# Transposes of a four-layer decoder trunk moved from TensorE to the DMA crossbar, and a second PSUM bank for gate and up

## The chip, the cores and the metric

One core of a Trainium2 chip. The time is device microseconds of one execution of the whole kernel; the figure of a kernel is the median of its runs. The profile comes from one more execution, under the hardware profiler.

## The reference

A decoder trunk of four layers on x of 256 rows and 1024 columns, all in float32. Layer i uses the mixer i mod 3, so the order is A, B, C, A:

```python
for i in range(DEPTH):                       # DEPTH 4
    hn = rms_norm(x, norm_gains[i, 0])
    m = mixer(hn)                            # A, B or C
    x = x + rms_norm(m, norm_gains[i, 1])
    f = swiglu(rms_norm(x, norm_gains[i, 2]), w_gate[i], w_up[i], w_down[i])   # hidden 2816
    x = x + rms_norm(f, norm_gains[i, 3])
# A: differential attention, 8 heads of two 64-wide maps, rotary positions, values 128 wide:
#    wts = softmax(q0 k0) - lam * softmax(q1 k1);  o = rms_norm(wts @ v, subln_g) * (1 - lam_init);  o @ w_out
# B: stick-breaking attention, 16 heads of 64, strictly causal:
#    a = exp(log_sigmoid(z) + sum over later keys of log_sigmoid(-z));  (a @ v) @ w_out
# C: sliding window of 128, 16 query heads on 2 key heads, learned sinks
```

## The kernel before

The 256 rows are two streams of 128 rows (s = 0 and 1). Both run the same program, `stream(s)`, as Python generators: a norm, the mixer, `out_proj`, a norm, `ffn`, a norm. Weights come in units of 128 x 1024 floats (512 KB), 378 in all. Each unit is loaded by SyncE's queue into one of STAGE = 4 buffers (`load_dma`, L247 and L251), split by ACT and DVE into a high and a low part (`hi`, `lo`), and held in a ring of 11; a product is three matmuls, high x high, high x low and low x high. Both streams use a unit once, so stream 0 may be at most LAG = 8 units ahead.

The class `Emitter` writes the order of the program: it keeps a clock of the matmul time emitted so far, lets the generators run in turn, and a generator says when it may go on: `("w",)` for the next weight unit, `("d", ns)` for a delay on that clock, `("e", key)` for an event that another sets. Work beside the main line (turning q, k, scores, values) is spawned as a task. After the first stretch the tile framework may still move an instruction ahead of one that waits. Nearly every instruction is recorded under one helper's line, L182, so the profile is read by tile names.

PSUM has 8 banks of 128 x 512 floats: for each stream one `tp` (transposes, values), one `mm` (projections), two `acc` (scores, output and down products, and the first chunk of a projection). Short-lived SBUF tiles share one ring of TMP = 8 buffers of 2 KB a partition (tag `t2k`).

A and B work in two groups g of four head pairs. For each group the units of q, k and v are projected in chunks of 512 columns (tiles `mm_a000q`: mixer, layer, stream, group, part). q and k are turned so that the head dimension lies on partitions: `four_transposes` makes four f32 transposes on TensorE into `tp` (tiles `tt_...`) and ACT copies them out (`qT`, `kT`). The scores (`sc_`) go through softmax or the stick-breaking scan in two steps of two; the weights of a step are turned the same way (`tw_`, `ta_`, copied to `wT`, `aT`), then the values are taken (`pv_`). A also normalises the output of each head and turns it (`on_`, `to_`). `split_rows` splits the result for `out_proj` (`acc_a`, `acc_b`), whose rows 0 to 3 come from the first group and 4 to 7 from the second.

`ffn` goes over 11 chunks of 256 hidden columns: `project` puts gate and up of a chunk side by side in one bank (`acc` for chunk 0, else `mm`; tile `mm_f`), ACT and DVE form h, h is turned, and `down` multiplies it into two `acc` banks (`acc_f`). Down of chunk c follows the projection of chunk c + 1; chunks 8, 9 and 10 come at the end. Except for the last chunk, h is turned by DMA, in `turned_by_dma` (L566): the crossbar moves two-byte elements, so GpSimd first copies the 32-bit words into planes of low and high halves (`hp`), SyncE's queue issues the transpose (`hq`), and GpSimd joins the halves (`hx`).

The gains of the two post norms of a layer are loaded for all partitions (`load_gain`, L447) into two buffers in turn, when stream 0 first needs them named.

Of the kernel before, what the change touches and what calls it, by code (L numbers as in the profile page):

```python
# [9 lines left out]
F32 = mybir.dt.float32  # L10
F32R = mybir.dt.float32r
BF16 = mybir.dt.bfloat16
I32 = mybir.dt.int32
U16 = mybir.dt.uint16
# [5 lines left out]
P = 128  # L20
D = 1024
# [13 lines left out]
TMP = 8  # L35
# [123 lines left out]
def trunk_kernel(ctx, tc, x, positions, norm_gains, a_w_in, a_w_out, a_lambda, a_subln, b_w_in, b_w_out,  # L159
# [285 lines left out]
    def load_gain(i, n):  # L445
        t = wk.tile([P, D], F32, tag="gain", name=f"gain_{i}_{n}")
        nc.sync.dma_start(t, norm_gains[i, n].partition_broadcast(P))  # L447
        return t

    gain_tiles = {}  # L450

    def gain_of(i, n):
        if (i, n) not in gain_tiles:
            gain_tiles[i, n] = load_gain(i, n)
        return gain_tiles[i, n]
# [40 lines left out]
    def project(s, xn, n, units_, name, first):  # L496

        b = bank("acc" if first else "mm", s, [P, n], f"mm_{name}")
        per = KT // units_
        for u in range(units_):  # L500
            w = yield ("w",)
            js = [(per * u + j, slice(j * n, (j + 1) * n)) for j in range(per)]
            for kt, cs in js:
                for v in range(2):
                    mm(b, xn[0][:, kt, :], w[v][:, cs], kt == 0 and v == 0, False)
            for kt, cs in js:
                mm(b, xn[1][:, kt, :], w[0][:, cs], False, kt == KT - 1)
        return b
# [52 lines left out]
    def turned_by_dma(h, name):  # L561

        planes = wk.tile([P, 2, 256], U16, tag="t2k", name=f"hp_{name}", bufs=TMP)
        pool.tensor_copy(planes, h.bitcast(U16).rearrange("p (n w) -> p w n", w=2))
        tq = wk.tile([P, 4, P], U16, tag="t2k", name=f"hq_{name}", bufs=TMP)
        nc.sync.dma_start_transpose(tq, planes.rearrange("p w n -> p (w n)"))  # L566
        t = wk.tile([P, 2, P], F32, tag="t2k", name=f"hx_{name}", bufs=TMP)
        pool.tensor_copy(t.bitcast(U16).rearrange("p b (t w) -> p w b t", w=2), tq.rearrange("p (w b) t -> p w b t", w=2))
        return t
# [14 lines left out]
    def layer_a(s, i, xn):  # L584
# [7 lines left out]
        def turned(chunk, g, which):  # L592
            t = rope(chunk, 8, *tabs[which], f"{name}{g}{which}")
            yield ("d", 2000)
            dst = None
            if which == "k":
                dst = kT[g, s] = wk.tile([P, 4, P], F32, tag=f"kT{g}{s}", name=f"kT_{name}{g}", bufs=1)
            else:
                dst = qT[g] = queries(s, 4, f"{name}{g}")
            four_transposes(s, t.rearrange("p h d -> p (h d)"), dst, f"tt_{name}{g}{which}")  # L600
            em.set((name, which, g))
            if which == "k":
                yield from scores(g)

        def scores(g):
# [8 lines left out]
            for step in range(3):  # L614
# [23 lines left out]
                if step > 0:  # L638
                    if step == 2:
                        yield ("d", 1500)  # L640
                    tp = bank("tp", s, [P, 2, nk, P], f"tw_{name}{g}{step}")
                    for h in range(2):
                        for kb in range(nk):
                            transpose(tp[:, h, kb, :], ws[step - 1][:, h, kb * P:(kb + 1) * P])
                    act.activation(wT[g][:, 2 * step - 2:2 * step], tp, AF.Copy)
                    yield ("d", 300)
# [4 lines left out]
        def values(g):  # L651
# [17 lines left out]
            tp = bank("tp", s, [P, 4, P], f"to_{name}{g}")  # L669
            for h in range(4):  # L670
                transpose(tp[:, h, :], on[:, h, :])
# [19 lines left out]
    def layer_b(s, i, xn):  # L691
# [6 lines left out]
        def turned(chunk, g, which):  # L698
# [8 lines left out]
            four_transposes(s, t, dst, f"tt_{name}{g}{which}")  # L707
# [4 lines left out]
        def scores(g):  # L712
# [6 lines left out]
            for step in range(3):  # L719
# [23 lines left out]
                if step > 0:  # L743
                    if step == 2:
                        yield ("d", 1500)
                    for p in range(2):
# [122 lines left out]
    def ffn(s, i, xn):  # L869
# [8 lines left out]
        def down(c):  # L878
            nonlocal acc
            for j in range(2):  # L880
# [6 lines left out]

        for c in range(NCH):
            chunk = yield from project(s, xn, 512, 4, f"{name}{c}", c == 0)
# [5 lines left out]
            if c == NCH - 1:  # L895
                yield from down(c - 2)
                yield from down(c - 1)
            elif c in (0, NCH - 2):
                yield ("d", 2200)
            else:  # L900
                yield from down(c - 1)
            if c == NCH - 1:
                t = bank("tp", s, [P, 2, P], f"th_{name}{c}")
                for j in range(2):
                    transpose(t[:, j, :], h[:, j * P:(j + 1) * P])
            else:
                t = turned_by_dma(h, f"{name}{c}")
            if c % 2 == 0:
                hT[c] = hT[c + 1] = [wk.tile([P, 4, P], F32R, tag=f"o{q}{s}", name=f"hT{q}_{name}{c}") for q in "hl"]
            split_rows(hT[c], slice(2 * (c % 2), 2 * (c % 2) + 2), t)  # L910
# [4 lines left out]
    def stream(s):  # L915
        if s:
            yield ("d", 1500)
        for i in range(depth):
# [6 lines left out]
            gain = gain_of(i, 1)  # L925
            oT, name = yield from (layer_a, layer_b, layer_c)[kind](s, i, xn)
            acc = yield from out_proj(s, oT, name, (1, 1, 3)[kind])
            post_norm(s, acc, gain, f"m{i}{s}")
            yield ("d", 4000)
            gain = gain_of(i, 3)  # L930
# [3 lines left out]
            post_norm(s, acc, gain, f"e{i}{s}")  # L934
            if i < depth - 1:
                yield ("d", 4000)
# [30 lines left out]
```

## Time and profile before

| | |
|---|---|
| median of 3 runs | 1188.63 us (1187.36 to 1189.47) |
| profiled execution | 1192.19 us, of which 1190.4 from first to last instruction |
| granted TensorE clock | 0.997 |
| TensorE (PE) busy | 1168.0 us (98%) |
| VectorE (DVE) busy | 779.4 us (65%) |
| ScalarE (ACT) busy | 649.0 us (55%) |
| GpSimd (POOL) busy | 175.0 us (15%) |
| moved by DMA | 216.42 MB, 182 GB/s in the mean |

PE stands for TensorE's matmuls (transposes among them), PEld for its weight loads, SP for SyncE. Matmuls are pipelined, so two of them overlap in the busy time, and what one costs the engine is read from start to start. A name in a row is that of the tile written, then, behind the arrow, those of the tiles read. The number behind x is a count. In a row of waits the numbers are total us, times, and where there is a third, the longest. In a timeline row they are start and length in us, and in brackets the engine's idle time before the instruction and what ended it.

### The profile page before, as it was taken

The page shows a single profiled execution, that of the slowest core. Times are in us where ns is not written, and L with a number is a line of the kernel's source. Part 1 is how long each engine was busy: PE and PEld are TensorE (multiplying, and loading weights), DVE is VectorE, ACT ScalarE, POOL GpSimd, SP SyncE. Part 2 cuts the span into 40 slices and gives each one's busy share as a digit, 9 for nine tenths or more (in the row PEclk, how much of TensorE's full clock was granted, in tenths as well). Part 3 has the DMA queues.
Part 4 walks back from the last instruction along what each step waited for, and adds up shares of the span by engine and source line. Part 5 has one row for each costly group of instructions (what it writes and reads, how often), then busy time and mean ns, then how long its engine had stood idle before and what let it go on. Part 6 is the DMA issues. An engine that isn't in the chain of part 4 may idle for free.

```text
span 1190.4 us, 16818 instructions
## 1 busy us (share of the span) xinstructions
PE 1168.0 (98%) x5868; PEld 958.5 (81%) x5868; DVE 779.4 (65%) x1217; ACT 649.0 (55%) x1197; POOL 175.0 (15%) x301
## 2 busy tenths in 40 slices
PE   8999999999999999999999999999999999999997
PEld 7787888888878888888888878888877888888776
DVE  7876765565847666666588676556686777655553
ACT  5665654444756665444476664444465666534542
POOL 2000122221200012111110012111110001211211
PEclk9999999999999999999999999999999999999999
DMA  8635467877743546777663256777764454677661
GB/s 278 211 124 161 147 193 195 225 211 216 233 135 125 177 145 196 213 208 226 207 203 125 90 158 201 210 209 212 217 207 144 139 162 130 193 205 215 192 194 40
DMA packets 184361, 216.42 MB, mean 182 GB/s; under 512 B 53074, under 2 KB 148436, under 8 KB 184276
## 3 DMA queue, kind: packets, MB, share of 16 engines
q1 hardware_dynamic: 183568, 215.00, 60.8%
q8 instruction: 46, 0.75, 0.3%
q10 hardware_dynamic: 708, 0.34, 0.1%
q14 instruction: 39, 0.32, 0.1%
HBM read 203.76 MB, written 1.05 MB: 172 GB/s over the span
## 4 chain that ended last, share of the span: by engine, by line
PE 68%; DMA 10%; DVE 7%; POOL 5%; ACT 5%; issue 4%; SPq 0%; POOLq 0%; ACTq 0%; DVEq 0%
PE mm_f L182 26%; PE acc_f L182 12%; DMA hq_f<-hp_f 8%; DVE lo L182 4%; PE acc_a L182 3%; POOL hp_f L182 3%; ACT hi L182 2%; PE mm_c L182 2%; PE acc_b L182 2%; PE sc_a L182 2%; POOL hx_f L182 1%; PE acc_c L182 1%; DMA stage<-in_a_w_in_dram 1%; PE sc_b L182 1%; PE pv_a L182 1%
## 5 line engine op out<-in xcount | busy, mean ns | idle before, releaser
L182 DVE TENSOR_TENSOR lo<-stage,hi 128x1024 fp32r<-128x1024 f32 x378 | 457.6, 1224 | 130.3 <-ACT hi L182 127.6
L182 ACT ACTIVATE hi<-stage 128x1024 fp32r<-128x1024 f32 x378 | 393.8, 1056 | 124.9 <-PE mm_f L182 49.9
L182 PE MATMUL mm_f<-hi,xh_q 128*128 128x512 f32 x704 | 275.8, 392 | 2.3 <-DVE h_f L182 2.3
L182 PE MATMUL mm_f<-lo,xh_q 128*128 128x512 f32 x704 | 274.8, 390 | 0.0
L182 PE MATMUL mm_f<-hi,xl_q 128*128 128x512 f32 x704 | 217.5, 390 | 1.0 <-DVE xl_q L182 1.0
L182 ACT ACTIVATE hTh_f<-hx_f 128x256 fp32r<-128x256 f32 x80 | 33.4, 418 | 229.4 <-POOL hx_f L182 229.4
L182 PEld LDWEIGHTS mm_f<-hi,xh_q 128*128 128x128 f32 x704 | 132.6, 188 | 30.9 <-ACT t_f L182 2.4
L182 PEld LDWEIGHTS mm_f<-hi,xl_q 128*128 128x128 f32 x704 | 132.4, 188 | 29.5 <-DVE xl_q L182 1.8
L182 PEld LDWEIGHTS mm_f<-lo,xh_q 128*128 128x128 f32 x704 | 132.6, 188 | 27.4 <-DVE lo L182 0.2
L182 DVE TENSOR_TENSOR hTl_f<-hx_f,hTh_f 128x256 fp32r<-128x256 f32 x80 | 34.0, 425 | 162.9 <-ACT hTh_f L182 162.9
L182 POOL COPY hp_f<-h_f 128x512 uint16<-128x512 uint16 x80 | 70.4, 880 | 301.5 <-DVE h_f L182 273.0
L182 PE MATMUL acc_f<-hi,hTh_f 128*128 128x512 f32 x352 | 111.3, 392 | 0.5 <-ACT hTh_f L182 0.5
L182 PE MATMUL acc_f<-lo,hTh_f 128*128 128x512 f32 x352 | 110.6, 390 | 0.7 <-DVE lo L182 0.5
L182 PE MATMUL acc_f<-hi,hTl_f 128*128 128x512 f32 x352 | 111.0, 391 | 0.0
L182 POOL COPY hx_f<-hq_f 128x512 uint16<-128x512 uint16 x80 | 62.8, 785 | 254.8 <-DMA hq_f<-hp_f 252.5
L182 PEld LDWEIGHTS acc_f<-lo,hTh_f 128*128 128x128 f32 x352 | 65.9, 188 | 15.2 <-DVE lo L182 1.5
L182 PEld LDWEIGHTS acc_f<-hi,hTh_f 128*128 128x128 f32 x352 | 65.7, 188 | 14.3 <-ACT hTh_f L182 0.8
L182 PEld LDWEIGHTS acc_f<-hi,hTl_f 128*128 128x128 f32 x352 | 65.8, 188 | 14.0 <-DVE hTl_f L182 0.5
L182 ACT ACTIVATE t_f<-mm_f,half_f 128x256 f32<-128x256 f32 x88 | 41.3, 469 | 59.6 <-PE mm_f L182 59.3
L182 DVE SCALAR_TENSOR_TENSOR t_f<-t_f,mm_f 128x256 f32<-128x256 f32 x88 | 36.6, 416 | 20.5 <-ACT t_f L182 20.4
L182 DVE SCALAR_TENSOR_TENSOR h_f<-t_f,hsq_f,mm_f 128x256 f32<-128x256 f32 x88 | 42.3, 480 | 2.9
L182 ACT ACTIVATE e_a<-sc_a,nm_a 128x128 f32<-128x128 f32 (+1 forms) x64 | 26.0, 420 | 17.0 <-DVE nm_a L182 16.9
(588 smaller groups left out, 1551.1 us busy)
## 6 DMA issues: line engine op xcount, KB each, us to landing
stage<-in_ffn_w_gate_dram SPq DMA_DIRECT2D x176, 256.0 KB, 3.1
stage<-in_ffn_w_up_dram SPq DMA_DIRECT2D x176, 256.0 KB, 3.8
stage<-in_ffn_w_down_dram SPq DMA_DIRECT2D x88, 512.0 KB, 4.5
stage<-in_a_w_in_dram SPq DMA_DIRECT2D x48, 512.0 KB, 4.5
stage<-in_b_w_in_dram SPq DMA_DIRECT2D x24, 512.0 KB, 4.1
stage<-in_a_w_out_dram SPq DMA_DIRECT2D x16, 512.0 KB, 3.7
stage<-in_c_w_in_dram SPq DMA_DIRECT2D x10, 512.0 KB, 4.1
gain<-in_norm_gains_dram SPq DMA_DIRECT2D x8, 512.0 KB, 4.5
```

The source lines that it names most:

```text
L182: i = call(*args, **kw)
```

## The change

In A and B the transposes of the first group (q, k, attention weights, and in A the output) and of q in the second group go through the crossbar, as h does in `ffn`: `by_dma` parts the halves and issues the transpose, and after a delay `words` joins them. Second-group k, weights and output stay on TensorE. In `ffn` a chunk's projection takes the banks `tp` and `mm` in turn, the turning of h is a task of its own (`turn`) that sets an event which `down` waits for, and the last chunk's two transposes use the `mm` bank. The norm gains have one buffer, loaded when stream 1's norm before it has been emitted; the space goes to TMP, now 10.

```diff
-TMP = 8
+TMP = 10
...
     def load_gain(i, n):
-        t = wk.tile([P, D], F32, tag="gain", name=f"gain_{i}_{n}")
+        t = gain_tiles[i, n] = wk.tile([P, D], F32, tag="gain", name=f"gain_{i}_{n}", bufs=1)
         nc.sync.dma_start(t, norm_gains[i, n].partition_broadcast(P))
...
+    def by_dma(src, n, name):
+        planes = wk.tile([P, 2, n * P], U16, tag="t2k", name=f"hp_{name}", bufs=TMP)
+        pool.tensor_copy(planes, src.bitcast(U16).rearrange("p (n w) -> p w n", w=2))
+        turned = wk.tile([P, 2, n, P], U16, tag="t2k", name=f"hq_{name}", bufs=TMP)
+        nc.sync.dma_start_transpose(turned.rearrange("p w b t -> p (w b) t"), planes.rearrange("p w n -> p (w n)"))
+        return turned
+
+    def words(dst, turned):
+        n = dst.shape[1]
+        pool.tensor_copy(dst.bitcast(U16).rearrange("p b (t w) -> p w b t", w=2),
+                         turned.rearrange("p w (b k) t -> p w b (k t)", b=n))
...  # layer_a and layer_b, turned()
-            four_transposes(s, t, dst, f"tt_{name}{g}{which}")
+            if g == 0 or which == "q":
+                halves = by_dma(t, 4, f"{name}{g}{which}")
+                yield ("d", 5500)
+                words(dst, halves)
+                yield ("d", 1500)
+            else:
+                four_transposes(s, t, dst, f"tt_{name}{g}{which}")
...  # layer_a, scores()
+                    if g == 0:
+                        halves = by_dma(ws[step - 1].rearrange("p h n -> p (h n)"), 2 * nk, f"{name}{g}w{step}")
+                        yield ("d", 5500)
+                        words(wT[g][:, 2 * step - 2:2 * step].rearrange("p h k t -> p h (k t)"), halves)
+                        yield ("d", 1500)
+                        continue
...  # layer_a, values()
-            tp = bank("tp", s, [P, 4, P], f"to_{name}{g}")
-            for h in range(4):
-                transpose(tp[:, h, :], on[:, h, :])
+            if g == 0:
+                halves = by_dma(on.rearrange("p h d -> p (h d)"), 4, f"{name}{g}o")
+                yield ("d", 5500)
+                tp = wk.tile([P, 4, P], F32, tag="t2k", name=f"to_{name}{g}", bufs=TMP)
+                words(tp, halves)
+                yield ("d", 1500)
+            else:
+                tp = bank("tp", s, [P, 4, P], f"to_{name}{g}")
+                for h in range(4):
+                    transpose(tp[:, h, :], on[:, h, :])
...  # layer_b, scores()
+                    if g == 0:
+                        halves = [by_dma(b.rearrange("p h n -> p (h n)"), 2 * nk, f"{name}{g}a{step}{j}")
+                                  for j, b in enumerate(as_[step - 1])]
+                        yield ("d", 6500)
+                        for j in range(2):
+                            words(aT[g][:, 2 * step - 2:2 * step, j].rearrange("p h k t -> p h (k t)"), halves[j])
+                        yield ("d", 2500)
+                        continue
...  # ffn
         def down(c):
             nonlocal acc
+            yield ("e", (name, "h", c))
...
+        def turn(c, h):
+            yield ("d", 2600)
+            turned = by_dma(h, 2, f"{name}{c}")
+            yield ("d", 4200)
+            if c % 2 == 0:
+                hT[c] = hT[c + 1] = [wk.tile([P, 4, P], F32R, tag=f"o{q}{s}", name=f"hT{q}_{name}{c}") for q in "hl"]
+            t = wk.tile([P, 2, P], F32, tag="t2k", name=f"hx_{name}{c}", bufs=TMP)
+            words(t, turned)
+            split_rows(hT[c], slice(2 * (c % 2), 2 * (c % 2) + 2), t)
+            em.set((name, "h", c))
+
         for c in range(NCH):
-            chunk = yield from project(s, xn, 512, 4, f"{name}{c}", c == 0)
+            chunk = yield from project(s, xn, 512, 4, f"{name}{c}", c == 0, ("tp", "mm")[c % 2])
...
-            if c == NCH - 1:
-                yield from down(c - 2)
-                yield from down(c - 1)
-            elif c in (0, NCH - 2):
-                yield ("d", 2200)
-            else:
-                yield from down(c - 1)
...
+            if c < NCH - 1:
+                em.spawn(turn(c, h))
+            for d in downs(c):
+                if d < NCH - 1:
+                    yield from down(d)
...  # stream
+            if i == 0 and s == 0:
+                load_gain(0, 1)
...
-            post_norm(s, acc, gain, f"m{i}{s}")
+            post_norm(s, acc, gain_tiles[i, 1], f"m{i}{s}")
+            if s:
+                load_gain(i, 3)
...
-            post_norm(s, acc, gain, f"e{i}{s}")
+            post_norm(s, acc, gain_tiles[i, 3], f"e{i}{s}")
             if i < depth - 1:
+                if s:
+                    load_gain(i + 1, 1)
```

More of the change, by code (lines that the diff above doesn't have):

```diff
@@ L445, in load_gain @@
     def load_gain(i, n):
-        t = wk.tile([P, D], F32, tag="gain", name=f"gain_{i}_{n}")
+        t = gain_tiles[i, n] = wk.tile([P, D], F32, tag="gain", name=f"gain_{i}_{n}", bufs=1)
         nc.sync.dma_start(t, norm_gains[i, n].partition_broadcast(P))
-        return t
     gain_tiles = {}
[L452 to L455, printed above, removed]
     def post_norm(s, acc, gain, name):
@@ L494, in out_proj, with project @@
         return acc
-    def project(s, xn, n, units_, name, first):
-        b = bank("acc" if first else "mm", s, [P, n], f"mm_{name}")
+    def project(s, xn, n, units_, name, first, tag="mm"):
+        b = bank("acc" if first else tag, s, [P, n], f"mm_{name}")
         per = KT // units_
@@ L559, in score_products @@
                 mm(sc[j][:, :, kb * P:(kb + 1) * P], identb, mask(kb).unsqueeze(1).to_broadcast([P, 2, P]), False, kb == kbs[-1])
[L561 to L569, printed above, removed]
+    def by_dma(src, n, name):
[8 more added lines that the diff above has]
+                         turned.rearrange("p w (b k) t -> p w b (k t)", b=n))
     def two_groups(s, name):
@@ L599, in turned @@
                 dst = qT[g] = queries(s, 4, f"{name}{g}")
-            four_transposes(s, t.rearrange("p h d -> p (h d)"), dst, f"tt_{name}{g}{which}")
+            t = t.rearrange("p h d -> p (h d)")
+            if g == 0 or which == "q":
[5 more added lines that the diff above has]
+                four_transposes(s, t, dst, f"tt_{name}{g}{which}")
             em.set((name, which, g))
@@ L706, in turned @@
                 dst = qT[g] = queries(s, 4, f"{name}{g}")
-            four_transposes(s, t, dst, f"tt_{name}{g}{which}")
+            if g == 0 or which == "q":
+                halves = by_dma(t, 4, f"{name}{g}{which}")
+                yield ("d", 5500)
+                words(dst, halves)
+                yield ("d", 1500)
+            else:
+                four_transposes(s, t, dst, f"tt_{name}{g}{which}")
             em.set((name, which, g))
@@ L894, in ffn @@
             dve.scalar_tensor_tensor(h, t, hsq, chunk[:, 256:512], ALU.mult, ALU.mult)
-            if c == NCH - 1:
-                yield from down(c - 2)
-                yield from down(c - 1)
-            elif c in (0, NCH - 2):
-                yield ("d", 2200)
-            else:
-                yield from down(c - 1)
[L902 to L910, printed above, removed]
+            if c < NCH - 1:
[3 more added lines that the diff above has]
+                    yield from down(d)
+        tp = bank("mm", s, [P, 2, P], f"th_{name}")
+        for j in range(2):
+            transpose(tp[:, j, :], h[:, j * P:(j + 1) * P])
+        hT[c] = [wk.tile([P, 4, P], F32R, tag=f"o{q}{s}", name=f"hT{q}_{name}{c}") for q in "hl"]
+        split_rows(hT[c], slice(2 * (c % 2), 2 * (c % 2) + 2), tp)
+        em.set((name, "h", c))
         yield ("d", 700)
@@ L924, in stream @@
                 act.on = dve.on = pool.on = pe.on = False
-            gain = gain_of(i, 1)
+            if i == 0 and s == 0:
+                load_gain(0, 1)
             oT, name = yield from (layer_a, layer_b, layer_c)[kind](s, i, xn)
             acc = yield from out_proj(s, oT, name, (1, 1, 3)[kind])
-            post_norm(s, acc, gain, f"m{i}{s}")
+            post_norm(s, acc, gain_tiles[i, 1], f"m{i}{s}")
+            if s:
+                load_gain(i, 3)
             yield ("d", 4000)
-            gain = gain_of(i, 3)
             xn = pre_norm(s, 4 * i + 2, f"q{i}{s}")
```

## The prediction

> **What bounds the kernel now.** I read the page's first part, then the busy time by stretch (cut by hand where the layers begin and end in the timeline), then TensorE's waits.
>
> ```profile
> span 1190.4 us, 16818 instructions
> PE 1168.0 (98%) x5868; PEld 958.5 (81%) x5868; DVE 779.4 (65%) x1217; ACT 649.0 (55%) x1197; POOL 175.0 (15%) x301
> ...
> 0.00:40.00 40.00, 34.61 (x169) 28.08 (x170) 31.55 (x60) 24.79 (x35) 8.23 (x57) 1.00 0.80 269
> 40.00:125.00 85.00, 83.32 (x470) 67.06 (x469) 60.34 (x103) 52.74 (x146) 4.19 (x6) 1.00 0.47 148
> 125.00:318.00 193.00, 191.92 (x855) 157.75 (x854) 121.59 (x172) 98.81 (x153) 40.47 (x51) 1.00 0.72 204
> 318.00:425.00 107.00, 106.87 (x654) 86.13 (x653) 69.42 (x108) 72.00 (x128) 6.23 (x24) 1.00 0.47 150
> 876.00:992.00 116.00, 114.63 (x637) 93.12 (x636) 87.49 (x160) 73.12 (x188) 7.36 (x12) 1.00 0.49 154
> ```
>
> The columns of a stretch are its length, then busy time of PE, PEld, DVE, ACT and POOL, the granted clock, the share of the DMA engines and GB/s. The reader is to see that PE has work all the time: in the attention of layer 0 (40 to 125) it is idle 1.7 us, of layer 1 (318 to 425) 0.1 us, of layer 3 (876 to 992) 1.4 us, at a granted clock of 1.00. Only the start is different: 5.4 us idle in 40, with DMA at 0.80 and 269 GB/s. In the same attention stretches POOL is busy 4 to 7 us and DMA half. So the span is PE's instructions laid end to end. An instruction taken off PE shortens it, as long as nothing PE then waits for comes late. The waits say what does so today:
>
> ```profile
> PE mm_f L182 <- DVE h_f L182: 2.3, 2, 2.0
> ...
> PE to_a L182 <- DVE on_a L182: 0.8, 1, 0.8
> ...
> PE acc_f L182 <- ACT hTh_f L182: 0.5, 1, 0.5
> PE acc_f L182 <- DVE lo L182: 0.5, 1, 0.5
> PE sc_a L182 <- ACT kT_a L182: 0.5, 1, 0.5
> ```
>
> These are total, count and longest of the waits. The 80 turns by DMA that the FFN already has cost PE 0.5 us in all (acc_f on hTh_f), because a whole chunk lies between a turn and its use.
>
> **Transposes off PE.** Counted from the code, for each stream: in the first kind of attention q of both groups and k of the first, 3 x 4 transposes; the first group's weights, 4 for stream 0 (one key block) and 8 for stream 1; the first group's output, 4. That is 44 a layer over both streams, 88 in layers 0 and 3. In the second kind (layer 1) 3 x 4 a stream, weights 8 and 16: 48. Together 136. What one is worth, by start to start of its group:
>
> ```profile
> 35.47 0.39 PE L182 MATMUL mm_a000v<-hi,xl_n 128*128 128x512 f32 x1
> 35.70 0.60 PE L182 MATMUL tt_a000k<-ident,t_a000k 128*128 128x128 f32 x4
> 36.05 0.47 PE L182 MATMUL mm_a000v<-hi,xl_n 128*128 128x512 f32 x1
> ...
> 62.53 0.66 PE L182 MATMUL to_a<-ident,on_a 128*128 128x128 f32 x4
> 63.12 0.37 PE L182 MATMUL sc_a<-kT_a,qT_a 64*128 64x128 f32 x1
> ```
>
> The columns are start, length, engine, line, operation, output and inputs, count. Four transposes move the next matmul from 35.70 to 36.05, so one costs 0.09 us, though each is busy longer (they are pipelined). 136 x 0.09 = 12.2 us. A group that waits for its input costs more: `to_a` takes 0.59 for four, 0.23 above its share. The 38 groups removed lie between 0 and 0.23 us of that; most look like the first, so I take 0.04 each, 1.6 us (0 to 8.7). This lies on the path, since PE is the path: **-13.8 us**. The ACT copies out of PSUM that go with the groups lie beside PE and save nothing.
>
> **Two banks for gate and up.**
>
> ```profile
> 1142.95 0.61 PE L182 MATMUL mm_f<-hi,xl_q 128*128 128x512 f32 x2
> 1145.57 0.56 PE L182 MATMUL mm_f<-hi,xh_q 128*128 128x512 f32 x1 [2.01 <-DVE h_f L182]
> ```
>
> With one bank, a chunk's first product waits for the vector engine's last read of the chunk before. Ordinarily the down product or the other stream covers that; where chunk 10 follows chunk 9 with no down product between and the other stream is in the same place, PE waits. That is the 2.3 us above: **-2.3 us** (0 to -2.3). The turn of h becomes a task of its own with two delays, and the down product now waits for its event; its cover is the next chunk, 24 matmuls, and the 0.5 us row bounds what gets past it. I take nothing.
>
> **What the turns cost elsewhere.** 38 crossbar transposes come in: 30 wide ones (128 x 1024 halves, 256 KB) and 8 of the present size. Each brings a POOL copy that parts the halves and one that joins them.
>
> ```profile
> L182 POOL COPY hp_f<-h_f x80: 606/613/1658, 135.5 to 1166.8; 128x512 uint16<-128x512 uint16 x80
> ...
> L182 POOL COPY hx_f<-hq_f x80: 757/763/1513, 138.8 to 1169.9; 128x512 uint16<-128x512 uint16 x80
> ...
> L566 SPq DMA_TRANSPOSE hq_f<-hp_f x80: 1194/1196/1872, 136.1 to 1167.4; - x80
> ...
> DMA to landing us min/median/max: 2.4/2.5/5.9
> ```
>
> These are minimum, median and maximum in ns; the last row counts from the issue on. Estimate for a wide turn, at double size: first copy 1.2 us (3.3 at the worst row), issue and transfer 2.5 to 5.0, second copy 1.5 (3.0), so 5.2 to 11.3 us. The slow level comes beside DVE:
>
> ```profile
> 298.90 1.23 DVE L182 TENSOR_TENSOR lo<-stage,hi 128x1024 fp32r<-128x1024 f32 x1
> ...
> 299.05 1.55 POOL L182 COPY hp_f<-h_f 128x512 uint16<-128x512 uint16 x1 [10.01 <-DVE h_f L182]
> ```
>
> This copy starts inside a subtraction with two SBUF inputs and takes 1.55 us where the median is 0.61; the subtraction's 1.23 us is its mean. So DVE, at 71% in layer 0's stretch and 65% in layer 1's, slows POOL and not the reverse. (The Trainium skill, SBUF — State Buffer, "Who interferes with whom", has it so: a DVE instruction with two SBUF inputs contends with a GpSimd one that reads SBUF, and the later of the two waits for the whole of the other. The pair of rows agrees; by that rule a POOL copy could also hold up DVE, which no row here shows.) POOL grows by about 30 x 2.7 + 8 x 1.4 = 93 us, to 270 of 1190: off the path.
>
> Now the path behind the first group. In layers 0 and 3 three turns follow one another (k, weights, output), in place of about 2.5 us each on PE and ACT (35.70 to 38.16 for k, whose copy is the first row below): 3 x (2.7 to 8.8) = 8 to 26 us later. Cover:
>
> ```profile
> 37.58 0.58 ACT L182 ACTIVATE kT_a<-tt_a000k 128x512 f32<-128x512 f32 x1
> ...
> 81.91 0.60 PE L182 MATMUL to_a<-ident,on_a 128*128 128x128 f32 x4
> ...
> 87.55 0.48 PE L182 MATMUL acc_a<-hi,oh_a 128*128 128x512 f32 x1
> ...
> 109.76 0.71 PE L182 MATMUL acc_a<-lo,oh_a 128*128 128x512 f32 x2
> ...
> 379.99 2.02 PE L182 MATMUL pv_b<-aT_b,V_b 128*64 128x128 f32 x32
> ...
> 406.43 0.70 PE L182 MATMUL acc_b<-hi,oh_b 128*128 128x512 f32 x2
> ```
>
> Stream 0's output is transposed at 62.53 and used at 87.55, 25.0 us later; stream 1's 81.91 and 109.76, 27.9; in layer 1 stream 1's values end near 382 and are used at 406.43, 24 us. So the output projection finds its rows ready, at nothing, unless nearly every step is at its worst; this cover is the second group's q, k and v, which stays.
>
> The exposed places are nearer: the first score product of the first group (it needs the turned k) and its first value product (the turned weights), 2 a stream and layer, 12. The code leaves 7 us of emitted PE work between turn and use; against 5.2 to 11.3 us PE waits 0 to 4.3 us. The nearest rows, PE's waits for kT_a and on_a above, are 0.5 and 0.8 us, once each over many such places. I take 0.25 each: **+3.0 us** (0 to 52).
>
> The start has no such cover:
>
> ```profile
> 29.67 1.06 ACT L182 ACTIVATE hi<-stage 128x1024 fp32r<-128x1024 f32 x1 [2.00 <-DMA stage<-in_a_w_in_dram]
> ...
> 38.21 0.72 PE L182 MATMUL sc_a<-kT_a,qT_a 64*128 64x128 f32 x8 [0.52 <-ACT kT_a L182]
> ```
>
> ACT waits for the weights as they land; three wide turns (q, k of stream 0, q of stream 1) now stand between them on the same queue, and the scores at 38.21 move to about 45. Price 0 to 3 x 2.6 = 8 us; stream 1, some units behind, has products to run meanwhile: **+1.5 us**.
>
> **SP and the norm weights.**
>
> ```profile
> SPq L247 <- DVE lo L182: 277.5, 119, 8.2
> SPq L566 <- POOL hp_f L182: 189.5, 76, 13.2
> ...
> SPq L447 <- DVE mg_e L182: 8.8, 3, 3.0
> ...
> SPq L447 <- DVE mg_m L182: 5.3, 3, 3.6
> ```
>
> SP mostly waits for a stage buffer, so it runs ahead of need, and has stood up to 13.2 us before a transpose without PE noticing. The number of norm loads stays 8; with one tile each waits for stream 1's norm, as six do now for 3 us or so. Queued behind are weight loads; their cover is the staged and split units, and PE's longest row for weights after the start is the 0.5 us of lo above. Nothing; if the cover goes, 7 x 3.6 = 25 us.
>
> **Sum.** -13.8 - 2.3 + 3.0 + 1.5 = -11.6 us. The profiled execution took 1192.2 us (span 1190.4 and 1.8 around it), 0.3% above the median; it would come to 1180.6, the median 1188.6 to **1177**. Without waits it would be 1172.5.
>
> **Rivals.** (1) *The turns come late, and it is slower.* PE stands at the 12 places because POOL's copy falls to its slow level and SP comes late. From 16.1 / 12 = 1.3 us a place it eats everything, start aside; at 2 us a place it is 1188.6 - 16.1 + 24 + 1.5 = 1198. For it: 3.3 us copies and the 5.9 us landing exist. Against: the FFN's 0.5 us. The Trainium skill speaks for this side: VectorE: DVE Perf Modes, "The three transpose paths" and the rules below it, lists 390 ns on TensorE and 1309 ns by the crossbar for one 128 x 128, and advises TensorE where PSUM will do. By that, 136 x 0.92 = +125 us (an estimate from the page) if all stood on the path; the 0.09 us of the rows is what PE really gives up, and what the crossbar costs off the path is free. (2) *Half or more is given back*: 0.7 to 1.0 us a place (3.0 becomes 8 to 12), or the start at its 8 us: 1182 to 1186. (3) *It doesn't do what it says*: PE isn't the limit in attention and its freed time turns idle, 1187 to 1190. Against it: 1.7, 0.1 and 1.4 us idle in the three stretches.
>
> **Chances.** Forecast (1169, with no waits and 0.13 us a group, to 1181) 0.64; given back 0.14; no change 0.07; slower 0.15. What a measurement tells here is about 0.2%, 2.4 us: faster 0.78, same 0.07, slower 0.15. The range reaches over rivals 2 and 3, 1169 to 1190, and leaves out most of the slower one.
>
> **What would show it.** PE's instructions fall by 136; its busy time by about 12; `tt_` and `tw_` groups remain for the second group only; the 2.0 us wait before chunk 10 is gone; POOL near 270 us. Wrong if PE's waits list sc_a, sc_b, pv_a or pv_b behind POOL with more than 10 us in all, or if the first stretch loses over 5 us more.

## The result, and the profile after

The changed kernel takes 1207.56 us (median of 4 runs, 1206.82 to 1210.47). The kernel before took 1189.05 us in 4 runs on the same chip. The ratio is 1.0158 (95% interval 1.0134 to 1.0181): slower by about 1.6%, where 1177 us had been forecast. The profiled execution took 1208.2 us.

The first part of the page and the busy time by stretch, with the columns as in the prediction; the last stretches begin and end a little later than those of before, with the work:

```profile
span 1206.4 us, 16604 instructions
PE 1161.5 (96%) x5732; PEld 950.5 (79%) x5732; DVE 812.2 (67%) x1217; ACT 636.8 (53%) x1163; POOL 311.3 (26%) x377
...
0.00:40.00 40.00, 34.03 (x156) 27.49 (x157) 30.48 (x55) 22.47 (x32) 12.78 (x60) 1.00 0.81 259
...
40.00:125.00 85.00, 76.62 (x393) 58.90 (x391) 62.80 (x101) 44.24 (x120) 30.70 (x24) 0.94 0.65 175
125.00:318.00 193.00, 191.81 (x863) 158.22 (x862) 122.28 (x167) 100.27 (x156) 47.54 (x52) 1.00 0.68 197
318.00:430.00 112.00, 103.70 (x582) 83.40 (x581) 83.46 (x105) 65.08 (x113) 42.02 (x50) 0.95 0.66 184
890.00:1010.00 120.00, 110.84 (x585) 88.77 (x585) 93.39 (x153) 66.63 (x176) 37.67 (x36) 0.97 0.63 172
```

PE lost its 136 instructions and 6.5 us of busy time, and stands idle far more: 8.4 us in the stretch of layer 0's attention (1.7 before), 8.3 in layer 1's (0.1) and 9.2 in layer 3's (1.4). Of the stretches shown, these three alone have a granted clock below 1.00. PE's waits name what it waits for (total, count, longest):

```profile
PE ta_b L182 <- DVE ol_b L182: 8.3, 1, 8.3
PE sc_a L182 <- POOL qT_a L182: 6.4, 2, 5.0
PE tp_q L182 <- DVE x L182: 2.5, 4, 1.1
...
PE sc_a L182 <- ACT e_a L182: 1.8, 2, 1.6
...
PE acc_a L182 <- ACT oh_a L182: 1.3, 1, 1.3
PE to_a L182 <- DVE on_a L182: 1.3, 2, 0.8
```

The wait of mm_f for h_f, 2.0 us before, is gone. Two waits, 8.3 and 5.0 us, are new. Behind or within waits the granted clock falls to one half. These are the four stretches of that before the last product, cut at the clock's steps:

```profile
52.90:59.70 6.80, 5.81 (x17) 4.02 (x16) 6.27 (x13) 1.74 (x7) 2.02 (x3) 0.50 0.57 180
100.70:104.10 3.40, 3.40 (x10) 2.63 (x9) 1.14 (x2) 0.00 (x0) 2.08 (x2) 0.50 1.11 315
390.90:401.10 10.20, 4.05 (x12) 3.27 (x13) 7.67 (x7) 1.45 (x3) 5.31 (x6) 0.50 0.41 107
974.50:981.30 6.80, 3.45 (x10) 2.66 (x11) 6.56 (x8) 3.31 (x4) 3.66 (x3) 0.50 0.74 205
```

They are 27.2 us long and PE is busy for 16.7 of them; at full clock that work would take half, so they cost some 8 us (an estimate from these rows; at most, since PE also waits in them). Before, there was one such stretch, right behind the 2.0 us wait:

```profile
1142.40:1145.80 3.40, 1.39 (x7) 0.88 (x6) 3.37 (x5) 2.28 (x4) 0.22 (x1) 1.00 0.65 199
1145.80:1149.20 3.40, 3.40 (x9) 2.64 (x9) 2.71 (x4) 1.06 (x1) 1.23 (x1) 0.50 0.82 289
```

Each stage's length, from the first transposes of stream 1's normed rows to the next such start (F3: to the start of PE's last product), in the profiled execution, shows where the time went. The letter is the kind of attention, F the FFN, the digit the layer; the labels e1 to e14 are those of the experiments below.

| | A0 | F0 | B1 | F1 | C2 | F2 | A3 | F3 |
|---|---|---|---|---|---|---|---|---|
| before | 132.4 | 176.5 | 122.0 | 175.5 | 90.0 | 176.9 | 122.0 | 175.3 |
| after | 139.9 | 176.0 | 127.8 | 175.5 | 90.1 | 177.1 | 128.8 | 170.3 |
| e1 | 133.5 | 176.0 | 123.9 | 175.5 | 90.3 | 177.1 | 122.7 | 170.3 |
| e2 | 139.7 | 176.0 | 123.5 | 175.5 | 90.1 | 177.2 | 123.7 | 170.3 |
| e3 | 139.4 | 176.0 | 123.4 | 175.5 | 90.0 | 180.3 | 127.1 | 170.3 |
| e4 | 133.8 | 176.5 | 126.4 | 175.1 | 91.9 | 177.5 | 125.3 | 170.7 |
| e5 | 131.9 | 176.1 | 120.6 | 175.5 | 90.0 | 177.1 | 130.4 | 170.3 |
| e6 | 133.5 | 176.1 | 123.3 | 175.6 | 90.0 | 177.1 | 123.9 | 170.2 |
| e7 | 139.5 | 176.0 | 119.7 | 175.5 | 90.0 | 177.1 | 129.1 | 170.2 |
| e8 | 132.4 | 176.0 | 122.1 | 175.4 | 89.5 | 177.1 | 122.0 | 170.8 |
| e9 | 137.6 | 176.0 | 127.9 | 175.5 | 90.0 | 177.1 | 124.7 | 170.3 |
| e10 | 135.7 | 176.1 | 122.8 | 175.6 | 90.1 | 177.1 | 123.1 | 170.2 |
| e11 | 133.3 | 176.0 | 123.0 | 175.5 | 90.1 | 177.1 | 122.7 | 170.3 |
| e12 | 132.6 | 176.0 | 119.8 | 178.9 | 89.5 | 177.2 | 122.0 | 170.1 |
| e13 | 133.0 | 176.0 | 123.1 | 175.5 | 90.0 | 177.3 | 122.6 | 170.3 |
| e14 | 144.1 | 176.0 | 126.7 | 175.5 | 90.1 | 177.1 | 130.6 | 170.3 |

After against before: +7.5, +5.8 and +6.8 us in the three attention stages with crossbar turns, -5.0 in the last FFN, about nothing elsewhere.

**The 5.0 us wait (layer 3).** POOL's queue, start and length, with its idle time in brackets:

```profile
968.16 1.35 POOL L182 COPY wT_a<-hq_a310w 128x1024 uint16<-128x1024 uint16 x1 [5.69 <-DMA hq_a310w<-hp_a310w]
969.43 1.96 POOL L182 TENSOR_TENSOR os_a<-os_a,mhalf 128x4 f32<-128x4 f32 x1
971.35 1.03 POOL L182 COPY hp_a311q<-t_a311q 128x1024 uint16<-128x1024 uint16 x1
...
975.57 2.23 POOL L182 COPY qT_a<-hq_a311q 128x1024 uint16<-128x1024 uint16 x1 [0.97 <-DMA hq_a311q<-hp_a311q]
```

and PE behind it:

```profile
972.27 0.63 PE L182 MATMUL to_a<-ident,on_a 128*128 128x128 f32 x4 [0.85 <-DVE on_a L182]
977.85 0.80 PE L182 MATMUL sc_a<-kT_a,qT_a 64*128 64x128 f32 x4 [4.96 <-POOL qT_a L182]
```

POOL takes its work in order. The join of the first group's weights stands at the head of its queue, waiting 5.7 us for a transfer; the parting of the second group's q, whose input was there at 967.3, starts only at 971.35. Its transfer and join follow, the join at POOL's slow level (2.23 us), and PE reaches the second group's scores before q is there. On PE and ACT, four such transposes and their copy took about 2.5 us (the prediction's rows for k).

**The 8.3 us wait (layer 1).** DVE's queue:

```profile
387.00 1.46 DVE L182 TENSOR_TENSOR b_b<-b_b,s_b 128x512 f32<-128x512 f32 x1
389.30 0.66 DVE L182 TENSOR_TENSOR b_b<-b_b,s_b 128x512 f32<-128x512 f32 x1
391.33 1.42 DVE L182 TENSOR_TENSOR b_b<-b_b,s_b 128x256 f32<-128x256 f32 x1
394.07 1.99 DVE L182 TENSOR_TENSOR lo<-stage,hi 128x1024 fp32r<-128x1024 f32 x1
...
396.32 0.68 DVE L182 TENSOR_TENSOR ol_b<-pv_b,oh_b 128x512 fp32r<-128x512 f32 x1
```

and POOL's and PE's:

```profile
391.08 2.85 POOL L182 COPY aT_b<-hq_b110a 128x1024 uint16<-128x1024 uint16 x2
...
393.85 1.14 POOL L182 COPY hp_b110a<-b_b 128x1024 uint16<-128x1024 uint16 x1
```

```profile
388.36 0.39 PE L182 MATMUL mm_b101v<-hi,xh_n 128*128 128x512 f32 x1
397.05 0.69 PE L182 MATMUL ta_b<-ident,b_b 128*128 128x128 f32 x2 [8.30 <-DVE ol_b L182]
```

ol_b is the last reader of a PSUM bank `tp`, which the second group's weights need. Its input pv_b was complete at 386.5 and oh_b at 387.1, but on DVE it stands behind the other stream's products and scans. The products run long beside POOL's copies: 1.46 for 128x512 against 0.66 for the same form, 1.42 for half of it, 1.99 for a `lo` whose mean was 1.22 before.

### The profile page after: what moved, and what is told of

It reads as the page before. It is cut to its first block, busy times and chain, and to the rows that moved or that the text cites. A ratio compares the mean times of both kernels' runs of the same rounds, so it can differ in the third digit from the quotient of the medians.

```text
span 1206.4 us, 16604 instructions
## 1 busy us (share of the span) xinstructions
PE 1161.5 (96%) x5732; PEld 950.5 (79%) x5732; DVE 812.2 (67%) x1217; ACT 636.8 (53%) x1163; POOL 311.3 (26%) x377
## 4 chain that ended last, share of the span: by engine, by line
PE 83%; DVE 6%; ACT 3%; DMA 3%; issue 2%; POOL 2%; SPq 0%; DVEq 0%; ACTq 0%; POOLq 0%
PE mm_f L182 38%; PE acc_f L182 19%; PE acc_a L182 3%; PE mm_c L182 2%; DVE lo L182 2%; PE acc_b L182 2%; PE acc_c L182 2%; DMA stage<-in_a_w_in_dram 1%; PE sc_a L182 1%; ACT hi L182 1%; PE sc_c L182 1%; PE sc_b L182 1%; PE mm_a010v L182 1%; ACT e_a L182 1%; DVE x L182 1%
## 5 line engine op out<-in xcount | busy, mean ns | idle before, releaser
L182 DVE TENSOR_TENSOR lo<-stage,hi 128x1024 fp32r<-128x1024 f32 x378 | 473.2, 1263 | 161.7 <-ACT hi L182 160.3
L182 POOL COPY hp_f<-h_f 128x512 uint16<-128x512 uint16 x80 | 90.3, 1129 | 410.8 <-DVE h_f L182 410.8
L182 POOL COPY hx_f<-hq_f 128x512 uint16<-128x512 uint16 x80 | 79.0, 987 | 86.5 <-DMA hq_f<-hp_f 86.0
L182 PEld LDWEIGHTS acc_f<-lo,hTh_f 128*128 128x128 f32 x352 | 66.1, 188 | 13.8
L182 PEld LDWEIGHTS acc_f<-hi,hTl_f 128*128 128x128 f32 x352 | 65.9, 188 | 13.8
```

The lines of the kernel that those rows point to most:

```text
L182: i = call(*args, **kw)
```

## The experiments

The theory was that the transposes come off PE as counted, but the turned rows reach PE late where nothing covers them, through POOL's order, the transfers and the clock that halves behind each wait. The rivals were that POOL's copies hold DVE up through the SBUF port that they share, that the FFN part or the single norm tile loses the time, and that SP's order does. Edits are against the changed kernel unless said otherwise. Times are medians, and a ratio is to the kernel before, run beside each. That kernel took 1191.2 us beside e1 to e4, 1189.1 beside e5 to e8, 1191.8 beside e9 to e12 and 1189.6 beside e13 and e14, so differences of less than some 3 us between runs of different groups say little.

### The parts alone: e1, e5, e6, e7, e10

e1 keeps the FFN part and the norm tile; all transposes of attention are on PE.

```diff
-            if g == 0 or which == "q":
+            if False:
...  # likewise, wherever `if g == 0:` chose the crossbar
```

> The attention's transposes all back on TensorE; the two banks for gate and up, the turn of h as a task, the one tile of norm weights and the ring of 10 stay. Theory H (the attention's turns come late, PE stands, and the granted clock halves behind each long wait): the 136 transposes return at 12 us, all waits of the attention go, and the FFN's own gain (5.4 us by the stages of the two traces) stays: 1181 to 1186. Rival F (the new FFN order, the single norm tile or the ring costs time too): 1190 or more. Granted clock back at 0.997 under H.

Measured: 1190.45 us, ratio 0.9994 (0.9979 to 1.0010). This missed. The last FFN is 5.0 us shorter, but A0, B1 and A3 are 1.1, 1.9 and 0.7 longer and nothing is left. So the attention part of the change costs 17.1 us by itself (19.5 by the two ratios). Around the start of each FFN PE has small waits: mm_f for hi (1.5 us in all, none before), acc_f for hTh_f (1.2, before 0.5) and tp_q for x (2.5, before 1.4). e1's timeline in layer 0:

```profile
145.11 0.49 PE L182 MATMUL mm_f<-hi,xh_q 128*128 128x512 f32 x1 [0.37 <-ACT hi L182]
145.83 0.50 PE L182 MATMUL acc_f<-hi,hTh_f 128*128 128x512 f32 x1 [0.22 <-ACT hTh_f L182]
146.76 0.41 PE L182 MATMUL tp_q<-ident,x 128*128 128x128 f32 x2 [0.43 <-DVE x L182]
```

e5 sends only q through the crossbar, e6 all but q, e7 all but layer 1's weights, e10 all but the second group's q.

```diff
-            if g == 0 or which == "q":   # e5, with the other branches False
+            if which == "q":
-            if g == 0 or which == "q":   # e6
+            if g == 0 and which == "k":
-                    if g == 0:           # e7, layer_b, scores()
+                    if False:
-            if g == 0 or which == "q":   # e10
+            if g == 0:
```

> The FFN part, and of the attention only q (both groups) by the crossbar: 12 turns; k, weights and output of the first group on TensorE. Theory H with every turn late on its own: the first group's scores still wait for the turned q, so about a third of the changed kernel's loss over the FFN part alone remains (17 us there, some 5 here: 1194 to 1197). Theory H with lateness only where turns follow one another (k, weights, output): 1187 to 1191. Rival P by number of copies (24 of 76, at 7.8 us for all): 2.5 us less the 4 us of 48 transposes, 1188 to 1190.

Measured: 1190.83 us, ratio 1.0011 (0.9996 to 1.0026). Against e1, layer 1 gains 3.3 us and layer 3 loses 7.7. The total lies where lateness only in chains of turns had put it (1187 to 1191), but the loss in layer 3 fits that poorly. There PE never waits for the turned q. It waits twice for on_a (3.3 us) and runs two stretches of 3.4 us at half clock; before the second of these waits DVE had a `lo` of 2.22 us beside POOL's join of q, and the chain to on_a stands behind it:

```profile
961.02 1.34 POOL L182 COPY qT_a<-hq_a311q 128x1024 uint16<-128x1024 uint16 x1 [4.02 <-PE pv_a L182]
961.17 2.22 DVE L182 TENSOR_TENSOR lo<-stage,hi 128x1024 fp32r<-128x1024 f32 x1 [0.15 <-ACT hi L182]
965.42 1.08 PE L182 MATMUL to_a<-ident,on_a 128*128 128x128 f32 x4 [1.62 <-DVE on_a L182]
```

> The changed kernel with all q on TensorE; k, weights and output of the first group stay on the crossbar (26 turns). Theory H with lateness in the chain of turns: 1200 to 1207, with the 8 us wait of ta_b for ol_b still there and the 5 us wait of sc_a for the turned q gone. If q was the late one: 1190 to 1195.

Measured: 1192.60 us, ratio 1.0024 (1.0012 to 1.0036), 15.0 below the changed kernel, as forecast for q as the late one. No stretch of half clock is left before the last 4 us, and PE is idle 3.0 and 3.7 us in the two later attention stages, against 9.2 and 8.3 in the changed kernel:

```profile
890.00:1010.00 120.00, 116.98 (x619) 94.45 (x618) 87.69 (x150) 67.13 (x171) 27.91 (x27) 1.00 0.55 162
318.00:430.00 112.00, 108.35 (x641) 86.60 (x640) 79.86 (x113) 68.92 (x122) 30.23 (x44) 1.00 0.57 166
```

> The changed kernel with the second kind's weights (layer 1) on TensorE again: 8 turns fewer. If the wait of ta_b for ol_b (8.3 us) and the 10 us at half clock behind it come from VectorE held up by the copies of those turns: layer 1's attention loses its 6 us over the kernel before and the whole is 7 to 13 us faster than the changed kernel, 1194 to 1200. If that wait comes from somewhere else (q and k turns, the ring of scratch tiles): 1204 to 1210.

Measured: 1199.23 us, ratio 1.0086 (1.0061 to 1.0111), 8.3 below the changed kernel. The wait of ta_b is gone and B1 falls from 127.8 to 119.7, below the 122.0 of before; the other stages stay. Layer 1's weights through the crossbar cost 8 us, its q and k gain 2 against the kernel before.

> The changed kernel with q of the second group on TensorE, q of the first still by the crossbar. If the second group's q is the late one, in the thick of the first group's joins: 1192 to 1197, near the 1192.6 with all q back. If the first group's q is it, at the head of the chain of turns: 1202 to 1208.

Measured: 1195.56 us (1192.06 to 1200.61), ratio 1.0036 (1.0016 to 1.0056), 12.0 below the changed kernel. The waits for qT_a are gone, ta_b's falls to 2.2 us, and in the profiled execution, the fastest of the nine (1192.06), A0, B1 and A3 give back 4.2, 5.0 and 5.7. Twenty-four transposes return to PE, and it is faster: of the pieces taken out singly, the second group's q is the costliest.

### What the added work costs without its use: e2, e3, e13

These start from e1 and spawn, at each of the 38 places, work whose result nobody uses; PE's transposes stay. e2 makes POOL's two copies, e3 also the crossbar transpose, e13 two memsets in place of the copies.

```diff
+            if g == 0 or which == "q":   # in layer_a and layer_b, and at the other places
+                em.spawn(shadow(t, 4, f"{name}{g}{which}"))
...
+        pool.tensor_copy(planes, ...)    # shadow(): e2; e13: pool.memset(planes, 0)
+        nc.sync.dma_start_transpose(...) # e3 alone
+        yield ("d", 5500)
+        words(dst, turned)               # e2, e3; e13: pool.memset(dst, 0)
```

> As the kernel with the FFN part alone, but at each of the 38 places where the changed kernel turns a tile, GpSimd also makes the two copies of a turn (parting and joining the halves) into scratch; no transfer, and nobody reads the result. Theory H: PE does not wait for these, so at most 3 us over the kernel without them. Rival P (GpSimd's copies hold up VectorE at the shared port and its own queue, and that alone makes PE wait): 10 us or more over it, with VectorE's busy time up by some 30 us as in the changed kernel (779 to 812).

Measured: 1198.22 us, ratio 1.0060 (1.0040 to 1.0081): 7.8 above e1, between the two forecasts, and mostly in A0 (+6.2). PE's waits that grew there are for results of DVE (w_a, t_a000k, on_a and rl_a: 6.0 us in all, in e1 1.8), none for POOL.

> As the one before, with the crossbar transposes too: everything a turn costs is there (copies, SyncE's issue, transfer), only nobody waits for the result, and TensorE keeps its 136 transposes. Theory H: within 4 us of the kernel with the FFN part alone, since lateness is the price and nothing is late for anyone. Rival D (the transposes stand ahead of weight loads on SyncE's queue and on the DMA engines, and PE runs out of weights): 8 us or more above the kernel with copies alone.

Measured: 1204.67 us, ratio 1.0121 (1.0082 to 1.0160): 6.5 above e2 and 14.2 above e1, so both forecasts missed. The 6.5 lie in F2 (+3.1) and A3 (+3.4). In F2, PE waits 2.2 us for xh_n and then runs 3.4 us at half clock; xh_n stands on ACT behind a weight unit that landed late (ACT idle for it 2.21 us, in e2 0.69):

```profile
887.36 1.06 ACT L182 ACTIVATE hi<-stage 128x1024 fp32r<-128x1024 f32 x1 [2.21 <-DMA stage<-in_a_w_in_dram]
888.32 2.15 ACT L182 ACTIVATE xh_n<-tp_n,gains 128x128 fp32r<-128x128 f32 x8
```

The last added turn before that is in layer 1, and the changed kernel's F2 is as long as e1's (177.1), so this part isn't shown to come from the transfers, and the change doesn't have it. In A3 PE has small waits for DVE's results (3.7 us in all, in e2 0.3; t_a301k 1.5); by which path the transfers or SP's issues cause them isn't shown.

> As the kernel with shadow copies, but each copy is replaced by a memset of the same scratch tile: GpSimd's queue is held about as long, but it reads nothing. Rival P (the port: GpSimd's reads against VectorE's second input): VectorE's mean subtraction back from 1.26 to 1.23 us and the 7.8 us gone, 1188 to 1192. If GpSimd's queue is what costs (the norm's powers and the FFN's copies behind the shadow work): 1196 to 1200, as with copies.

Measured: 1189.48 us, ratio 0.9986 (0.9965 to 1.0007): e1's time. The group of `lo` subtractions, of e1, e2 and e13 in turn (columns: count, busy us and mean ns, idle time before):

```profile
L182 DVE TENSOR_TENSOR lo<-stage,hi 128x1024 fp32r<-128x1024 f32 x378 | 459.7, 1226 | 164.4 <-ACT hi L182 162.2 <-DMA stage<-in_ffn_w_down_dram 0.2
```

```profile
L182 DVE TENSOR_TENSOR lo<-stage,hi 128x1024 fp32r<-128x1024 f32 x378 | 471.5, 1260 | 151.5 <-ACT hi L182 150.2
```

```profile
L182 DVE TENSOR_TENSOR lo<-stage,hi 128x1024 fp32r<-128x1024 f32 x378 | 460.6, 1229 | 162.7 <-ACT hi L182 160.9
```

Copies on POOL, which read SBUF, stretch DVE's two-input subtractions; memsets, which don't, leave them alone. DVE's busy time says the same: 784.4 in e1, 812.0 in e2, 784.5 in e13. With PE's waits in e2, which are for DVE and not for POOL, this puts the copies' 7.8 us on DVE, which they hold up, and not on POOL's queue. The comparison has a gap: the memsets add 61 us to POOL (271.6 against 210.6), the copies 102, and a memset waits for no source.

### The copies on another engine: e4, e9, e14

```diff
-        pool.tensor_copy(dst...., turned....)                # e4: every join
+        act.activation(dst...., turned...., AF.Copy)
...  # e9: both copies of q on ACT; e14: both copies of all 38 turns on ACT
```

> The changed kernel with the joining copy (of the attention and of the FFN) on ScalarE instead of GpSimd; ScalarE is busy 53%. Theory H with GpSimd's queue as the cause of lateness (a join that waits for its transfer holds the next parting copy and the norm's power behind it): 8 to 15 us faster than the changed kernel, 1192 to 1199. If the lateness is that of the transfer alone: 1204 to 1210, as changed. Rival P: also faster, since half of the copies that share VectorE's port go, but then VectorE's mean subtraction of a weight unit falls back to 1.22 us from 1.26.

Measured: 1198.18 us, ratio 1.0062 (1.0044 to 1.0080), 9.4 below the changed kernel. A0 falls by 6.1 and A3 by 3.5; ta_b's wait is 5.2 us. DVE's `lo` falls only part of the way, to 1236 ns, and ACT, which now makes the joins, goes from 636.8 to 740.9 us.

> The changed kernel with both copies of every q turn on ScalarE, the other turns as they are. The q of the second group stood behind the joins and powers in GpSimd's queue. If that queue is the cause: the 5.0 us wait of sc_a for qT goes and most of the 15 us that taking q off the crossbar gave back comes too, 1192 to 1198. If it is the transfer and SyncE's queue: 1203 to 1209.

Measured: 1200.90 us, ratio 1.0073 (1.0045 to 1.0100), 6.7 below, between the two forecasts. A3 falls by 4.1, the wait of sc_a from 5.0 to 2.4 us, but ta_b still waits 7.2.

> The changed kernel with both copies of every attention turn on ScalarE; the FFN's stay on GpSimd, the transfers and delays are unchanged. If GpSimd's port and queue are the cause: 1186 to 1193, a gain of 14 us or more, with VectorE's mean subtraction at 1.23 us. If the transfers (6 us and more from issue to landing, on SyncE's queue behind weight loads) make the turns late by themselves: 1197 to 1205.

Measured: 1210.09 us, ratio 1.0154 (1.0109 to 1.0200). This missed: DVE is relieved (782.9 us, `lo` at 1225 ns), POOL too (210), and it is as slow as the change. The waits are now behind ACT's order:

```profile
PE sc_a L182 <- ACT qT_a L182: 5.3, 1, 5.3
PE acc_a L182 <- ACT oh_a L182: 3.6, 2, 3.0
```

The port alone is therefore not the cause. In both orders that were tried, POOL's and ACT's, the copies stand in front of something that PE needs, or behind it.

### The FFN part: e8, e11, e12

e8 is the kernel before with one bank exchanged: the last chunk is projected into `tp` and its transposes go to `mm`. e12 adds layer 1's q by crossbar. e11 is e1 with two norm tiles and TMP at 8.

```diff
-            chunk = yield from project(s, xn, 512, 4, f"{name}{c}", c == 0)
+            chunk = yield from project(s, xn, 512, 4, f"{name}{c}", c == 0, "tp" if c == NCH - 1 else "mm")
...  # e8, against the kernel before
-                t = bank("tp", s, [P, 2, P], f"th_{name}{c}")
+                t = bank("mm", s, [P, 2, P], f"th_{name}{c}")
```

> The kernel before with one edit: chunk 10 of an FFN takes the bank tp in place of mm, and its two transposes mm. The 2.0 us wait before chunk 10 of the last FFN and the 3.4 us at half clock behind it go: 3 to 4 us faster than before (the last FFN of the changed kernel was 5 us shorter), 1185 to 1188. If the changed FFN's gain at the end came from the turn as a task instead: no change.

Measured: 1186.29 us, ratio 0.9974 (0.9962 to 0.9986). As forecast. In the profiled executions F3 is 4.5 us shorter, and no stage is longer by more than 0.2; by the medians the gain is 2.9 us. The row of the place where the kernel before waited and then ran at half clock:

```profile
1141.00:1151.00 10.00, 10.00 (x46) 8.26 (x45) 6.23 (x9) 4.00 (x7) 2.74 (x3) 1.00 0.81 229
```

> The FFN part alone, with norm weights in two buffers and a ring of 8 as before. The FFN part gained 5 us in the last FFN and lost 4 in the stages before. If the single tile of norm weights holds up SyncE's queue behind stream 1's norm and costs those 4 us: 1184 to 1187. If the turn as a task does: 1189 to 1192.

Measured: 1189.77 us, ratio 0.9990 (0.9975 to 1.0005), as e1: neither the norm tile nor the ring of 10 is what the FFN part loses by.

> The kernel before with chunk 10 in the other bank, and layer 1's q of both groups by the crossbar (4 turns, 16 transposes off TensorE); nothing else. Layer 1's attention with q alone by the crossbar took 3 us less than without, and POOL is nearly idle there: 1182 to 1186. If a turn is late when next to few others too: 1187 or more.

Measured: 1186.00 us (1183.24 to 1192.20), ratio 0.9953 (0.9933 to 0.9973), with an interval that overlaps e8's, at the upper end of what was forecast. B1 gains 2.2 us, but in the profiled execution F1 loses 3.4: from 611.5 acc_f waits 2.1 us for hTl_f, and the clock is halved behind it.

```profile
611.00:614.80 3.80, 1.69 (x8) 1.08 (x7) 3.80 (x5) 2.66 (x8) 0.00 (x0) 1.00 0.77 237
614.80:618.20 3.40, 3.40 (x15) 3.00 (x14) 3.18 (x10) 2.86 (x8) 0.84 (x2) 0.50 0.97 348
```

Both e8 and e12 beat the kernel before and the changed one; which is the better is not settled.

## Why the prediction was wrong

Its first rival came true, that the turns come late and the kernel gets slower, but not at the 12 places that the rival priced, and its 1198 us was too cheap. By the prediction's steps:

**Transposes off PE, -13.8: right.** The count fell by 136. From e1 to the changed kernel PE's busy time fell by 4.6 us (1166.1 to 1161.5), although half clock adds some 8 us to it: about 13 us of work did leave PE, by these estimates. e6 needs no such correction: neither it nor e1 has half clock before the last 4 us, and with 88 transposes fewer PE is busy 7.6 us less, 0.09 each as the prediction had it; 136 come to some 12.

**Two banks, -2.3: right in mechanism, too small, and paid back.** e8 gives 4.5 us in that stage (2.9 by the medians). Behind the 2.0 us wait the prediction overlooked 3.4 us at half clock, in the trace of before; the wait was priced, the clock behind it was not. The rest of the FFN part gives about 4 us back in the attention stages (e1). It isn't the norm tile (e11). The turn as a task or two banks for all chunks could be the reason; neither was tried alone.

**"The exposed places", +3.0: the step that failed.** Three things were wrong in it.
- *The list.* It held the first group's scores and values, at 0.25 us each. There the changed kernel shows no wait of PE for a turned tile. The waits stand elsewhere: at the second group's scores (sc_a on qT_a, 5.0 and 1.5 us) and at the second group's transposes of weights in layer 1 (ta_b on ol_b, 8.3). With q back on PE (e6), PE has no wait of more than 1.3 us in attention, though the first group's k, weights and output still take the crossbar. The output projection's cover, priced at nothing, held but in one place. In layer 0 stream 0's turned output was ready 33.7 us later than before (96.9 against 63.2), more than the 8 to 26 that were forecast for the chain of three turns and than the cover of 25.0, and PE's acc_a waits 1.3 us for oh_a (first row below). What was missed is that a turn also delays others: on POOL's queue the join of one turn stands, waiting for a transfer, before the parting of the next, and on DVE the reader that frees a bank stands behind stretched products. The second group's q, moved in the same edit, was priced as a transpose saved.
- *"DVE slows POOL and not the reverse".* POOL slows DVE as well: `lo` from 1224 to 1263 ns in the mean, DVE from 779.4 to 812.2 us, and e2 puts 7.8 us on the copies, which e13 doesn't have. The Trainium skill, SBUF — State Buffer, "Who interferes with whom", says that a DVE instruction with two SBUF inputs contends with a GpSimd one that reads SBUF, and that issue order decides who waits. The trace agrees, with 1.46 and 0.66 us for the same product, and with e13, where memsets don't disturb. The prediction had the rule and set its second half aside, because "no row here shows" it. The trace of before does have such rows: three of its 378 `lo` take over 1.3 us, each beside a POOL copy, and the longest, 1.68 us, begins just after one (last rows below). In the changed kernel there are 26.
- *The clock.* There was no term for it. Half-clock stretches of 27.2 us cost at most some 8 us by the estimate above. Their share was not separated by a run of its own.

The row of the turned output in layer 0 of the changed kernel:

```profile
96.91 0.72 ACT L182 ACTIVATE oh_a<-to_a,gsub 128x512 fp32r<-128x512 f32 x1 [3.06 <-POOL to_a L182]
```

A `lo` stretched beside a POOL copy, in the kernel before:

```profile
1043.92 0.61 POOL L182 COPY hp_f<-h_f 128x512 uint16<-128x512 uint16 x1 [5.91 <-DVE h_f L182]
1043.94 1.68 DVE L182 TENSOR_TENSOR lo<-stage,hi 128x1024 fp32r<-128x1024 f32 x1
```

**SP and the transfers, nothing: not borne out, but not sized.** Of the 6.5 us that e3 adds, the 3.4 in A3 may be theirs; the 3.1 in F2 have no counterpart in the changed kernel. The wide turns were issued in the 1.2 us of the narrow ones (medians), and landed 3.0, 4.0 and 6.1 us later (minimum, median, maximum), within the 2.5 to 5.0 that had been estimated but for the end; the FFN's own rose from 2.5 to 3.3. The two turns of one name in layer 3, with the time to landing counted from the issue:

```profile
L560 SPq DMA_TRANSPOSE hq_a310w<-hp_a310w x2: 1232/1234/1237, 962.0 to 974.6; - x2
...
DMA to landing us min/median/max: 3.7/4.9/6.1
```

**POOL 270 us, "off the path": too low, and on the path** (the 5.0 us wait). It came to 311.3, since the FFN's copies too run at the slow level more often (median 1544 ns, 613 before; e1, without the other turns, already has POOL at 210.6):

```profile
L182 POOL COPY hp_f<-h_f x80: 609/1544/1648, 142.9 to 1182.6; 128x512 uint16<-128x512 uint16 x80
```

**The start, +1.5: not far off.** The first scores came at 46.0, where the prediction had about 45, and the first 40 us lose 0.6 us of PE's work; the loss in A0 comes later, with its waits and half clock.

**The sign it named, too narrow.** It would be wrong if PE's waits behind POOL came to over 10 us. They came to 6.4; the other 8.3 stood behind DVE, so a watch on POOL's name alone would have missed the larger half.

From e1, the sum reads: -12 (transposes) + 7.8 (copies, e2) + 3.4 (transfers, at most what e3 adds in A3) gives -0.8, so some 18 us stay for lateness and the clock, where the prediction had 3.0 and nothing. These terms overlap: e4, e7, e9 and e10 give back 9.4, 8.3, 6.7 and 12.0 us, more than there is in all. That PE stands late is seen in the trace (8.3 and 5.0 us), and e6, e7 and e10 show which turns bring it about. But they take out the copies and transfers of these turns too, so how much of it is lateness of the turned rows, how much DVE held up and how much the clock stays open.

## What to carry to other kernels

When work is moved from the engine that bounds the kernel to one that is idle, price the lateness and not the busy time: for each result that moves, list what stands before it on every in-order queue it passes, and what is queued behind an instruction that now waits for a transfer. Move first what has most cover, one kind at a time; here one bank for one chunk (e8) was worth more than the whole change. Around each wait of about 2 us, look up the granted clock in the slices behind it, since that is part of its price.

## What the runs showed of the hardware

- The granted clock fell to one half behind waits of about 2 us: 2.0 us at 1143.6 (before), 2.1 at 611.5 (e12). The stretches last 3.4, 6.8 or 10.2 us. The Trainium skill, TensorE: Matmul & The Clock Gate, "What's actually happening", gives a free-running window of 3413 ns; the lengths agree. In "Why this matters for your kernels" it names idle gaps above about 3 us as what brings the clock down; here shorter ones did, with PE busy for 1.39 of the 3.4 us before (the row of before). That busy time doesn't decide alone: in the changed kernel PE was busy 2.17 us of 49.5 to 52.9 and the clock fell, in e2 1.63 us of 45.6 to 49.0 and it stayed. What else decides isn't shown.
- POOL and DVE stretch one another: a POOL copy of 128x512 from 0.61 to 1.5 us, and a DVE subtraction of 128x1024 from 1.22 to 2.07 (at 968.45 in the changed kernel, beside the join at 968.16).
- A crossbar transpose of twice the width was issued in the same 1.2 us in the median, and landed 4.0 us after its issue.
